# The residual kept by token: 512 moving weight columns per product, and seams pipelined by halves of the tokens

## The chip, the cores and the metric

The kernel runs on one core of a Trainium2 chip. The metric is the time of one execution on the device, in microseconds; several runs are taken and the median counts. A profiled execution gives the trace: TensorE (PE, with its weight loads as PEld), VectorE (DVE), ScalarE (ACT), GpSimd (POOL), and the queues of the DMA engines, most of whose transfers SyncE (SP) issues.

## What is computed

256 tokens of 1024 features go through two blocks, in float32. Cut to what matters:

```python
# block 1
h = swiglu(rms_norm(x, g1), w_in, w_out)            # 1024 -> 2 x 2816 -> 1024, silu(gate) * up
x = x + 0.5 * rms_norm(h, g2)
m = token_mixing(rms_norm(x, g3), ...)              # 4-head retention, 8-head neighbourhood attention, gates, projection
x = x + rms_norm(m, g4)
x = x + 0.5 * rms_norm(swiglu(rms_norm(x, g5), ...), g6)
# block 2, layers i = 0, 1 (0: causal attention of 16 heads; 1: differential attention of 8)
shift1, scale1, gate1, shift2, scale2, gate2 = split(silu(c) @ ada_w[i] + ada_b[i], 6)
y = attention(x * (1 + scale1) + shift1)
x = layer_norm(sqrt(2) * x + (1 + gate1) * y, ln_g[i, 0], ln_b[i, 0])
y = square(relu((x * (1 + scale2) + shift2) @ w_up[i])) @ w_down[i]      # 1024 -> 4096 -> 1024
x = layer_norm(sqrt(2) * x + (1 + gate2) * y, ln_g[i, 1], ln_b[i, 1])
```

The seven parts are FFN1, mixing, FFN2, attention 0, MLP 0, attention 1, MLP 1. What lies between two of them is called a seam here: a norm over the features of what the part gave, the new residual, and the input of the next part.

## The kernel before

**Products.** A float32 value is split into two float32r parts, high and low, and a product of two float32 matrices is three products of parts: high·high, low·high, high·low. All weights are streamed once: 198 slots of 1 MB, each in two halves. `Stream` loads a slot into `raw` (4 buffers, SP's queue), ACT copies a half into `wh` (line 109), DVE subtracts to get `wl` (line 90), and 7 halves of each can be in stock (RING). After each half slot that TensorE uses up, `tick()` emits the split of the next halves and advances the generators (`gens`) that hold the attention's and the sums' work, so that the order on every engine is that in which the program writes its instructions; nothing reorders them later. Instructions of an engine run in that order, and a waiting one holds up those behind it.

**Layout.** The residual X lies by features: [128 features, 8 chunks, 256 tokens], and nearly all products (`mmB`) hold a 128x128 block of weights stationary and move the 256 tokens (`g`, `u`, `q`, `k`, `acc` and so on: 48 products a slot). The values of attentions and mixing (`projA`) hold 128 tokens stationary and move 256 weight columns. In MLP up, after an attention, 258 columns are moved: two more columns carry what the norm's mean and shift add (`Ahead`).

**Seams.** Sums over the features run across partitions, so they are made with products against ones (`Stat.mms`, banks `pst`), after POOL or DVE have added six chunks; the factor 1/deviation (POOL's pow) is spread over partitions by two more products (`bcast`, banks `MU` and `R`); XH and XL, the parts of the next input, follow by chunks. Into these gaps the program puts one-column products of adaptive sums (`ada_mm`) and products that nobody reads (`warm`), both through `gap`. From an attention to its MLP the first products run before the statistics are known, on the unnormalized v.

**Adaptive sums.** silu(c) @ ada_w: 12 vectors of 1024, whose weights come as 48 more slots between the others. DVE adds up raw times a scalar (`adacc`, lines 317 and 320), then ACT and POOL make three bfloat16 parts (lines 331 to 337), and 24 one-column products (bank `adp`) add up the partitions. 9 of the 12 (HELD) have them in seams.

Of the kernel before, what the change touches and what calls it, by code (L numbers as in the profile page):

```python
# [16 lines left out]
D = 1024  # L17
S = 256
# [15 lines left out]
# the order of the parts of an attention (1 for queries and keys, 0 for values; of which heads), after how  # L34
# many steps of the stream a pair of heads starts, and from which pair on two of its steps are one
QKV = (((1, 0), (0, 0), (0, 1), (1, 1), (1, 2), (1, 3), (0, 2), (0, 3)),
       ((1, 0), (0, 0), (1, 1), (1, 2), (0, 1), (1, 3), (0, 2), (0, 3)))
WAITS = ((4, 5, 4, 3, 0, 5, 2, 1), (6, 5, 2, 4, 4, 4, 0, 2))
ONE = ((7, 8), (8, 6))
RET_WAITS = (1, 3, 4, 9)  # L40
NA_WAITS = (3, 2, 5, 4)

# the sums whose last products wait for the gap between two parts
HELD = (0, 1, 2, 4, 5, 6, 7, 9, 10)
# [5 lines left out]
class Stream:  # L50
    """Weights in the order of their use: loaded ahead, split into two float32r parts ahead."""
# [19 lines left out]
    def load(self, i, q=None):  # L71
# [3 lines left out]
        t = self.raw[i].rearrange("p (a b) -> p a b", b=s[2])  # L75
        if q is None:
            self.nc.sync.dma_start(t, s[1])
        else:
            n = t.shape[1] // 4
            self.nc.sync.dma_start(t[:, q * n:(q + 1) * n], s[1][:, q * n:(q + 1) * n])  # L80
# [41 lines left out]
    def quarter(self, n, q):  # L122
        """A quarter of slot n, the first of which come before any others."""
        h, c = q // 2, slice(q % 2 * 512, q % 2 * 512 + 512)
        if q % 2 == 0:
            self.parts[n, h] = tuple(self.pool.tile([128, 1024], F32R, name=i, bufs=RING) for i in ("wh", "wl"))
        wh, wl = self.parts[n, h]
        raw = self.raw[n][:, q * 512:(q + 1) * 512]
# [12 lines left out]
    def ahead(self):  # L141
        """The next half of a slot, when it is a weight's."""
# [3 lines left out]
    def use(self, n, b):  # L146
        """Slot n in two halves of its rows; each as its two parts, b columns wide."""
# [14 lines left out]
def block_kernel(ctx, tc, A, out):  # L162
# [22 lines left out]
    def rev(t):  # L185
        """[128, 2, 256] of a tile, every 64 of a row backwards."""
# [6 lines left out]
    # ---- small tensors  # L193
    xn = big.tile([128, 2, D], F32, name="xn", tag="P1")
# [5 lines left out]
    def first_loads(st):  # L200
        sy = nc.sync
        sy.dma_start(cst[:, 0:256], A["head"])
        for q in range(4):
            sy.dma_start(xn[:, :, q * 256:(q + 1) * 256], xv[:, :, q * 256:(q + 1) * 256])
            for i in range(2):
                st.load(i, q)
# [34 lines left out]
    def ffn_slots(w_in, w_out):  # L241
        def up(j):
            ws.append(cols(w_in, 256 * j))
            ws.append(cols(w_in, DFF + 256 * j))
        order(DFF // 256, up, lambda j: ws.append(rws(w_out, 256 * j)))

    def mlp_slots(w_up, w_dn):
        n = DFF2 // 256
        for j in range(n + 3):
# [7 lines left out]
    for i in range(2):  # L257
        ws.append(cols(wm, 256 * i))
        ws.append(cols(wm, 512 + 256 * i))
        for j in (2 * i, 2 * i + 1):  # L260
            ws.append(cols(wm, 1024 + 256 * j))
        for j in (2 * i, 2 * i + 1):
            ws.append(cols(wm, 2048 + 256 * j))
    for i in range(2):
        for b in (3072, 3584, 4096):
            ws.append(cols(wm, b + 256 * i))
    for i in range(4):
        ws.append(cols(wm, 4608 + 256 * i))
        ws.append(cols(A["w_ret_out"], 256 * i))
    for i in range(2):  # L270
        ws.append(cols(wm, 5632 + 512 * i))
        ws.append(cols(wm, 5632 + 512 * i + 256))
        ws.append(cols(A["w_na_out"], 512 * i, n=512))
# [3 lines left out]
    for l, (wi, wo) in enumerate((("moba_w_in", "moba_w_out"), ("diff_w_in", "diff_w_out"))):  # L277
        for f, i in QKV[l]:
            for b in ((0, D) if f else (2 * D,)):
# [1460 lines left out]
```

## Time and profile before

| | |
|---|---|
| median of 3 runs | 1287.63 us (1287.5 to 1288.11) |
| span of the profiled execution | 1287.8 us |
| TensorE busy | 1262.7 us, 98% |
| VectorE busy | 1046.8 us, 81% |
| ScalarE busy | 672.0 us, 52% |
| GpSimd busy | 280.5 us, 22% |
| read from memory | 262.56 MB, 205 GB/s over the span |

The profiled execution's span is all that is recorded of its time; it is the time that sums are made against. Busy shares are means over parts with different limits, so what a change is worth is read from the stretch in which it stands.

### The profile page before, as it was taken

Reading aid. Unit: us, or ns where it says so; the run is one execution under the profiler, and the core shown is the slowest. Engines: PE = TensorE matmul, PEld = TensorE weight load, DVE = VectorE, ACT = ScalarE, POOL = GpSimd, SP = SyncE. Lnnn points to the kernel's source line nnn. Section 1 sums busy time; section 2 is a strip of 40 time slices with the busy share of each in tenths; the row PEclk is TensorE's granted clock in tenths of the full one; section 3 lists DMA queues with packets and bytes.
Section 4 is the critical chain, followed back from the end, with each engine's and each line's share of the span. In section 5 each row is a group of like instructions: output and inputs, shape, how many; then the busy total and the mean of one; then the engine's idle time right before and its main releaser. Section 6 shows DMA issues by size and latency. Waiting matters only on the chain.

```text
span 1287.8 us, 25632 instructions
## 1 busy us (share of the span) xinstructions
PE 1262.7 (98%) x10768; PEld 1244.6 (97%) x10768; DVE 1046.8 (81%) x1437; ACT 672.0 (52%) x1070; POOL 280.5 (22%) x204
## 2 busy tenths in 40 slices
PE   9999999999999999999999999979999999999998
PEld 9999999999999999999999999979999999999997
DVE  5999867887776589887588759999969987998864
ACT  5454445656544365354465546545536565565542
POOL 1011104221000130011110017423322003832311
PEclk9999999999999999999999999989999999999999
DMA  8787974874566348877535335878753543677630
GB/s 300 264 309 256 317 244 90 268 240 149 200 226 212 116 164 301 303 279 262 164 111 186 131 99 188 270 271 281 260 171 113 183 132 103 225 250 234 202 134 33
DMA packets 176659, 265.25 MB, mean 206 GB/s; under 512 B 10432, under 2 KB 145952, under 8 KB 176544
## 3 DMA queue, kind: packets, MB, share of 16 engines
q1 hardware_dynamic: 169824, 261.53, 60.1%
q10 hardware_dynamic: 6720, 2.10, 0.9%
q8 instruction: 84, 1.38, 0.4%
q14 instruction: 31, 0.25, 0.1%
HBM read 262.56 MB, written 1.05 MB: 205 GB/s over the span
## 4 chain that ended last, share of the span: by engine, by line
PE 86%; DVE 8%; POOL 2%; issue 1%; ACT 1%; DMA 0%; DVEq 0%; SPq 0%; POOLq 0%; ACTq 0%
PE acc L191 24%; PE u L191 20%; PE g L191 12%; PE v L191 3%; PE q L191 3%; PE k L191 3%; PE oacc L191 2%; DVE wl L90 2%; PE yr L191 2%; PE rg L191 2%; PE rv L191 2%; PE as L191 1%; PE ao L191 1%; PE pst L191 1%; PE nk L191 1%
## 5 line engine op out<-in xcount | busy, mean ns | idle before, releaser
L90 DVE TENSOR_TENSOR wl<-raw,wh 128x1024 fp32r<-128x1024 f32 x392 | 515.2, 1334 | 24.3 <-ACT wh L109 23.9
L109 ACT ACTIVATE wh<-raw 128x1024 fp32r<-128x1024 f32 x392 | 403.6, 1052 | 130.3 <-PE u L191 32.2
L191 PE MATMUL acc<-HL,wh 128*128 128x256 f32 x864 | 243.9, 282 | 0.0
L191 PE MATMUL acc<-HH,wl 128*128 128x256 f32 x864 | 243.7, 282 | 0.0
L191 PE MATMUL acc<-HH,wh 128*128 128x256 f32 x864 | 242.8, 281 | 0.0
L191 PE MATMUL u<-XH,wh 128*128 128x258 f32 (+1 forms) x864 | 201.6, 285 | 0.4 <-ACT wh L129 0.4
L191 PE MATMUL u<-XL,wh 128*128 128x258 f32 (+1 forms) x864 | 200.7, 284 | 0.0
L191 PE MATMUL u<-XH,wl 128*128 128x258 f32 (+1 forms) x864 | 200.2, 283 | 0.0
L191 PEld LDWEIGHTS acc<-HH,wh 128*128 128x128 f32 x864 | 163.9, 190 | 0.0
L191 PEld LDWEIGHTS acc<-HH,wl 128*128 128x128 f32 x864 | 162.4, 188 | 0.0
L191 PEld LDWEIGHTS acc<-HL,wh 128*128 128x128 f32 x864 | 161.9, 187 | 0.0
L191 PEld LDWEIGHTS u<-XH,wh 128*128 128x128 f32 x864 | 145.7, 191 | 0.7 <-ACT wh L129 0.6
L191 PEld LDWEIGHTS u<-XH,wl 128*128 128x128 f32 x864 | 146.0, 191 | 0.1
L191 PEld LDWEIGHTS u<-XL,wh 128*128 128x128 f32 x864 | 145.1, 190 | 0.0
L191 PE MATMUL g<-XH,wh 128*128 128x256 f32 x480 | 133.5, 284 | 1.6 <-ACT XH L942 1.3
L191 PE MATMUL g<-XL,wh 128*128 128x256 f32 x480 | 133.2, 283 | 1.0 <-DVE XL L618 0.9
L191 PE MATMUL g<-XH,wl 128*128 128x256 f32 x480 | 132.7, 282 | 0.0
L320 DVE SCALAR_TENSOR_TENSOR adacc<-raw,csil,adacc 128x1024 f32<-128x1024 f32 x84 | 118.2, 1408 | 1.7
L834 POOL TENSOR_TENSOR a<-a,RB 128x512 f32<-128x512 f32 x32 | 68.0, 2125 | 170.7 <-DVE a L833 169.9
L333 POOL TENSOR_TENSOR adacc<-adacc,ada 128x1024 f32<-128x1024 f32 x12 | 27.7, 2311 | 329.3 <-ACT ada L331 254.3
L191 PEld LDWEIGHTS g<-XH,wh 128*128 128x128 f32 x480 | 89.5, 189 | 2.7 <-ACT XH L942 2.0
L191 PEld LDWEIGHTS g<-XL,wh 128*128 128x128 f32 x480 | 89.5, 189 | 1.6 <-DVE XL L618 1.1
(368 smaller groups left out, 2643.0 us busy)
## 6 DMA issues: line engine op xcount, KB each, us to landing
raw<-in_ada_w_dram SPq DMA_DIRECT2D x48, 1024.0 KB, 5.7
raw<-in_ffn_w_in_dram SPq DMA_DIRECT2D x42, 1024.0 KB, 6.8
raw<-in_mlp_w_up_dram SPq DMA_DIRECT2D x32, 1024.0 KB, 5.4
raw<-in_mlp_w_down_dram SPq DMA_DIRECT2D x32, 1024.0 KB, 5.0
raw<-in_w_mix_in_dram SPq DMA_DIRECT2D x26, 1024.0 KB, 5.6
raw<-in_ffn_w_out_dram SPq DMA_DIRECT2D x22, 1024.0 KB, 5.8
raw<-in_moba_w_in_dram SPq DMA_DIRECT2D x12, 1024.0 KB, 5.2
raw<-in_diff_w_in_dram SPq DMA_DIRECT2D x12, 1024.0 KB, 5.1
```

The costliest lines, as they stand in the source:

```text
L90: self.nc.vector.tensor_tensor(wl, raw, wh.bitcast(F32), OP.subtract)
L109: nc.scalar.activation(wh, self.raw[i][:, sl], AF.Copy)
L191: PE.matmul(o, l, r, start=start, stop=stop, skip_group_check=True)
L320: V.scalar_tensor_tensor(t, w, csil[:, kb:kb + 1], t, op0=OP.mult, op1=OP.add)
L333: GP.tensor_tensor(t, t, parts[0], OP.subtract)
L834: GP.tensor_tensor(two(t), two(t), bc2(self.R), OP.mult)
```

## The change

The residual now lies by token: X is [128 tokens, 2, 1024], and XX = [128 features, 8, 2 (high, low), 256] is the part's input, turned. Most products are now of one form, `mmA`: 128 tokens of an input stationary, 512 weight columns moving, 24 products a slot; slots are loaded as 512 columns of four chunks (`wide`), or 256 gate and 256 up columns (`both`). Queries, keys, the mixing's rq, rk, nq, nk, MLP up from block 2 on, and the late values of the attentions keep 256 columns. Sums over the features are now along a row: ACT's squares with a running sum (RMS), or DVE's `bn_stats` (layer norm). Gains, biases and gates that vary along a row come as rows broadcast by DMA (15 of 0.5 MB). Since hidden values are made by token, they are turned with TensorE transposes: 4 for a block of an FFN, 16 in an MLP, 16 in the mixing.

In a seam `down_tail` finishes token half 0 (accumulators (0, 0), (0, 1)), then half 1; `bank(t, f)` normalizes; `mid()` puts the transposes of half 0 (`turn(0)`, 8) where 6 products of half 1 are left; `projT` then does the next part's first 24 products for half 0, `turn(1)`, and 24 for half 1. `gap`, `warm` in seams, the statistics' products and `Ahead` are gone. Adaptive sums are emptied by `spare` within the parts: 8 of 12 as 24 one-column products, the 4 gates (s of 2 and 5) as 6 products of 512 columns that spread the sum over partitions. Their order among the weights, and the order and waits of the attentions' parts (QKV, WAITS, RET_WAITS), change too.

The core of the diff (of the new functions what is spoken of; what was removed is in the kernel above):

```diff
+QKV = (((2, 0), (1, 0), (1, 1), (1, 2), (1, 3), (0, 2), (0, 3)),
+       ((2, 0), (1, 0), (1, 1), (1, 2), (1, 3), (0, 2), (0, 3)))
+WAITS = ((0, 1, 0, 1, 0, 1, 0, 1), (0, 1, 0, 1, 0, 1, 0, 1))
 ONE = ((7, 8), (8, 6))
...
+    def wide(w, c0, k=KB):
+        return [("w", w[r:r + 512, c0:c0 + 512].rearrange("(k p) f -> p k f", p=128), 512) for r in range(0, 128 * k, 512)]
+    def both(w, c0):
+        v = w.rearrange("(k p) (g f) -> p k g f", p=128, g=2)
+        return [("w", v[:, k:k + 4, :, c0:c0 + 256], 512) for k in (0, 4)]
...
+    adas = [(l, s, i) for l, s in ((0, 0), (0, 1), (0, 3), (0, 4), (1, 0), (0, 2), (0, 5), (1, 1), (1, 3), (1, 4), (1, 2),
+                                   (1, 5)) for i in range(4)]
...
+    def spare(p):
+        if not ada_out:
+            return
+        l, s, parts, h = ada_out[0]
+        if s in (2, 5):
+            if h is None:
+                h = 0
+                g = grows[l, s] = late.tile([128, D], F32, name="grow", bufs=2)
+                src = A["ada_b"]
+                nc.sync.dma_start(g, bass.AP(tensor=src.tensor, offset=src.offset + (6 * l + s) * D, ap=[[0, 128], [1, D]]))
+            ada_out[0] = (l, s, parts, h + 1)
+            if h == 1:
+                ada_out.pop(0)
+            c = slice(512 * h, 512 * h + 512)
+            for i in range(3):
+                mm(p, onesb.to_broadcast([128, 128]), parts[i][:, c], i == 0, i == 2)
+            yield 1
+            g = grows[l, s][:, c]
...
+    def mmA(o, wh, wl, x, s, e):
+        mm(o, x[:, 0], wh, s, False)
+        mm(o, x[:, 0], wl, False, False)
+        mm(o, x[:, 1], wh, False, e)
+    TS = (slice(0, 128), slice(128, 256))
...
+    def projA(banks, X, nk=KB):
+        for i in range(nk // 4):
+            n = nxt()
+            for h, (wh, wl) in enumerate(st.use(n, 512)):
+                for t in range(2):
+                    for k in range(2):
+                        kk = 4 * i + 2 * h + k
+                        mmA(banks[t], wh[:, k], wl[:, k], X[:, kk, :, TS[t]], kk == 0, kk == nk - 1)
+                st.release(n, h)
+                tick()
+    def projT(banks, turn):
+        ns = [nxt(), nxt()]
+        w = []
+        for t in range(2):
+            turn(t)
+            for i in range(2):
+                if t == 0:
+                    w.append(st.use(ns[i], 512))
+                for h, (wh, wl) in enumerate(w[i]):
+                    for k in range(2):
+                        kk = 4 * i + 2 * h + k
+                        mmA(banks[t], wh[:, k], wl[:, k], XX[:, kk, :, TS[t]], kk == 0, kk == 7)
+                    if t:
+                        st.release(ns[i], h)
+                    if t or h:
+                        tick()
+    def down(accs, H, first):
         n = nxt()
         for kk, (wh, wl) in enumerate(st.use(n, D)):
+            for t in range(2):
+                for f in range(2):
+                    fs = slice(512 * f, 512 * f + 512)
+                    mmA(accs[t][f], wh[:, 0, fs], wl[:, 0, fs], H[:, kk, :, TS[t]], first and kk == 0, False)
             st.release(n, kk)
             tick()
+    def down_tail(accs, hs, post, mid):
         ns = [nxt(), nxt()]
         w = [st.use(n, D) for n in ns]
+        for t in range(2):
+            for f in range(2):
+                fs = slice(512 * f, 512 * f + 512)
+                for i in range(2):
+                    for kk in range(2):
+                        wh, wl = w[i][kk]
+                        mmA(accs[t][f], wh[:, 0, fs], wl[:, 0, fs], hs[i][:, kk, :, TS[t]], False, i == 1 and kk == 1)
+                    if t and f and i == 0:
+                        mid()
+                if t and f:
+                    for n in ns:
+                        for h in range(2):
+                            st.release(n, h)
+                post.bank(t, f)
+                if not (t and f):
+                    tick()
...
+    def turn_of(src, a, c, alloc=gu):
+        def turn(t):
+            for b in range(2):
+                p = alloc("xt")
+                for i in range(4):
+                    PE.transpose(p[:, i * 128:(i + 1) * 128], src[:, t, (4 * b + i) * 128:(4 * b + i + 1) * 128], ident)
+                f = None if c is None else w2("hf")
+                for i in range(4):
+                    k = 4 * b + i
+                    x, h, l = p[:, i * 128:(i + 1) * 128], XX[:, k, 0, TS[t]], XX[:, k, 1, TS[t]]
+                    if c is None:
+                        SC.activation(h, x, AF.Copy, scale=a[:, k:k + 1])
+                        V.scalar_tensor_tensor(l, x, a[:, k:k + 1], h.bitcast(F32), op0=OP.mult, op1=OP.subtract)
+                    else:
+                        ff = f[:, i * 128:(i + 1) * 128]
+                        SC.activation(h, x, AF.Identity, scale=a[:, k:k + 1], bias=c[:, k:k + 1])
+                        V.tensor_scalar(ff, x, a[:, k:k + 1], c[:, k:k + 1], op0=OP.mult, op1=OP.add)
+                        V.tensor_tensor(l, ff, h.bitcast(F32), OP.subtract)
...
     class PostRms:
+        def bank(self, t, f):
+            squares(self.s[:, t, f:f + 1], self.accs[t][f])
+            self.m[t, f] = w2("m")
+            V.tensor_tensor(self.m[t, f], self.accs[t][f], half(self.gain, f), OP.mult)
+            if f:
+                c = 1.0 / (self.coef * self.coef)
+                s = self.s[:, t, 0:1]
+                V.tensor_tensor(s, s, self.s[:, t, 1:2], OP.add)
+                r = rcol(s, c, D, self.eps)
+                for f in range(2):
+                    x = half(X[:, t], f)
+                    V.scalar_tensor_tensor(x, self.m.pop((t, f)), r, x, op0=OP.mult, op1=OP.add)
...
     class PostLn:
+        def bank(self, t, f):
+            v = half(self.v[:, t], f)
+            V.tensor_tensor(v, self.accs[t][f], half(self.gate, f), OP.mult)
+            V.scalar_tensor_tensor(v, half(X[:, t], f), ALPHA, v, op0=OP.mult, op1=OP.add)
+            V.bn_stats(self.s[:, t, f], v)
+            if f:
+                V.bn_aggr(self.mv[:, t], self.s[:, t].rearrange("p f s -> p (f s)"))
+                e = work.tile([128, 1], F32, name="ve", bufs=2)
+                V.tensor_scalar(e, self.mv[:, t, 1:2], 0.0, LN_EPS, op0=OP.max, op1=OP.add)
+                self.norm(t, self.mv[:, t, 0:1], rpow(e))
+        def norm(self, t, mu, r):
+            n = work.tile([128, 1], F32, name="nm", bufs=2)
+            V.scalar_tensor_tensor(n, mu, -1.0, r, op0=OP.mult, op1=OP.mult)
+            SC.activation(half(self.v[:, t], 0), half(self.v[:, t], 0), AF.Identity, scale=r, bias=n)
+            V.tensor_scalar(half(self.v[:, t], 1), half(self.v[:, t], 1), mu, r, op0=OP.subtract, op1=OP.mult)
...
+    def swiglu(cx, gain, first, post, mid):
...
+        def hidden(j, ps):
+            a, b = w2("a"), w2("b")
+            for t in range(2):
+                SC.activation(two(a)[:, t], ps[t][:, 0:256], AF.Silu, scale=r[0][:, t:t + 1])
+            for t in range(2):
+                V.scalar_tensor_tensor(two(b)[:, t], ps[t][:, 256:512], r[0][:, t:t + 1], two(a)[:, t],
+                                       op0=OP.mult, op1=OP.mult)
+            yield 1
+            p = ps[0]
+            for c in range(2):
+                for t in range(2):
+                    PE.transpose(two(p)[:, c, TS[t]], two(b)[:, t, c * 128:(c + 1) * 128], ident)
+            H = hp.tile([128, 2, 2, S], F32R, name="H", bufs=4)
+            split(H[:, :, 0], H[:, :, 1], two(p))
+            hid[j] = H
+            yield from spare(ps[1])
+            yield from spare(ps[0])
...
```

The first place is TensorE in FFN1, from the last product of block 2's projection into the first of its down product. Before (H is the hidden's two parts HH and HL, u the up projection):

```order
L191 MATMUL u<-XL,wh 128x256
L191 MATMUL u<-XH,wl 128x256
L191 MATMUL acc<-HH,wh 128x256
L191 MATMUL acc<-HL,wh 128x256
L191 MATMUL acc<-HH,wl 128x256
```

Of the change, at the same place (ps[0] and ps[1] are both named g; cst holds the identity):

```order
L197 MATMUL g<-wh,XX 128x512 x2
L197 MATMUL g<-wl,XX 128x512
L197 MATMUL g<-wh,XX 128x512
L197 MATMUL acc<-wh,H 128x512
...
L197 MATMUL acc<-wh,H 128x512
L695 MATMUL g<-cst,b 128x128 x4
L197 MATMUL acc<-wh,H 128x512
L197 MATMUL acc<-wl,H 128x512
```

Products have twice the columns, and four transposes of b stand in the middle of the down slot, 12 products behind the projection whose results they need.

The second place is VectorE in the seam from attention 0 to MLP 0 (oacc is the attention's output product, four banks; wl are low parts of the MLP's first weights). Before:

```order
L654 SCALAR_TENSOR_TENSOR v<-oacc,g_7816,X 128x256 x4
L761 SCALAR_TENSOR_TENSOR XL<-v,m00a,XH 128x256 x2
L777 TENSOR_TENSOR vs<-v 128x512
L90 TENSOR_TENSOR wl<-raw,wh 128x1024
L654 SCALAR_TENSOR_TENSOR v<-oacc,g_7816,X 128x256 x2
L761 SCALAR_TENSOR_TENSOR XL<-v,m00a,XH 128x256 x2
L779 TENSOR_TENSOR vs<-vs,v 128x512
...
L783 TENSOR_TENSOR ssum<-vs 128x256
L90 TENSOR_TENSOR wl<-raw,wh 128x1024 x3
```

Of the change, from the norm of half 0 on (hf and XX at lines 584 and 585 come 8 times each in turn):

```order
L631 SCALAR_TENSOR_TENSOR nm<-mv,r 128x1
L633 TENSOR_SCALAR v<-v,mv,r 128x512
L620 TENSOR_TENSOR v<-oacc,grow 128x512
L621 SCALAR_TENSOR_TENSOR v<-X,v 128x512
L622 BN_STATS bs<-v 128x6
...
L584 TENSOR_SCALAR hf<-xt,m00a,m00c 128x128
L585 TENSOR_TENSOR XX<-hf,XX 128x128
...
L620 TENSOR_TENSOR v<-oacc,grow 128x512
...
L633 TENSOR_SCALAR v<-v,mv,r 128x512
L96 TENSOR_TENSOR wl<-raw,wh 128x1024 x4
```

The second bank of half 1 now stands behind all of half 0's parts, and the next weights' low parts behind half 1's norm, which waits for POOL's pow; on ACT the order is the same (norm of half 1, then four copies `wh`).

## Rows read from the trace of the kernel before

**Rows 1.** The page: the span, each engine's busy time, the chain by engine.
```profile
span 1287.8 us, 25632 instructions
...
PE 1262.7 (98%) x10768; PEld 1244.6 (97%) x10768; DVE 1046.8 (81%) x1437; ACT 672.0 (52%) x1070; POOL 280.5 (22%) x204
...
PE 86%; DVE 8%; POOL 2%; issue 1%; ACT 1%; DMA 0%; DVEq 0%; SPq 0%; POOLq 0%; ACTq 0%
```

**Rows 2.** The chain in order of time, in FFN1: start, duration, engine, what.
```profile
46.20 5.68 PE acc L191 x48
51.88 5.70 PE g L191 x48
```

**Rows 3.** MLP 0's stall: TensorE's timeline, the chain, a window (columns as in rows 7).
```profile
845.46 0.74 PE L191 MATMUL adp<-small,ada 128*128 128x1 bf16 x22 [5.63 <-POOL ada L337]
...
846.20 5.14 PE u L191 x24
851.34 5.75 PE acc L191 x48
...
838.00:850.00 12.00, 5.42 (x48) 5.15 (x48) 11.89 (x13) 5.06 (x7) 5.24 (x2) 0.61 0.66 213
```

**Rows 4.** TensorE's timeline in mixing and its first seam; the tail's chain.
```profile
242.59 1.89 PE L191 MATMUL ry<-rv,dec 128*128 128x256 f32 x8
200.81 1.08 PE L191 MATMUL pst<-small,sq 128*128 128x64 f32 x8
...
1278.90 0.88 PE fo L863 x8
```

**Rows 5.** Seams: TensorE's timeline FFN1 to mixing, MLP 0 to attention 1; its waits.
```profile
199.71 0.66 PE L191 MATMUL pst<-small,ssum 128*128 128x64 f32 x4
204.91 0.47 PE L191 MATMUL rq<-XH,wh 128*128 128x256 f32 x2 [0.22 <-DVE XH L614]
207.03 0.51 PE L191 MATMUL rq<-XL,wh 128*128 128x256 f32 x2 [0.93 <-DVE XL L618]
...
966.33 1.24 PE L191 MATMUL pst<-small,ssum 128*128 128x64 f32 x8
972.42 0.50 PE L191 MATMUL q<-XH,wh 128*128 128x256 f32 x2
...
PE pst L191 <- DVE ssum L783: 1.9, 2, 1.0
```

**Rows 6.** Groups by line and form (busy, mean ns, idle before); two pieces of the chain.
```profile
L320 DVE SCALAR_TENSOR_TENSOR adacc<-raw,csil,adacc 128x1024 f32<-128x1024 f32 x84 | 118.2, 1408 | 1.7
L654 DVE SCALAR_TENSOR_TENSOR v<-oacc,g,X 128x256 f32<-128x256 f32 x16 | 7.0, 476 | 5.3 <-PE oacc L191 5.3
L1581 DVE TENSOR_SCALAR o<-ao,r 128x128 f32<-128x128 f32 x16 | 4.9, 347 | 0.3
...
L587 ACT ACTIVATE sq<-acc 128x512 f32<-128x512 f32 x9 | 5.4, 598 | 14.6 <-PE acc L191 14.6
L1276 ACT ACTIVATE ry<-ry,r 128x256 f32<-128x256 f32 x8 | 3.3, 464 | 1.8 <-POOL r L540 1.8
...
L337 POOL TENSOR_TENSOR ada<-adacc,ada 128x1024 bf16<-128x1024 f32 x12 | 33.1, 2756 | 30.1 <-ACT ada L335 30.1
L540 POOL TENSOR_TENSOR r<-s,small 128x2 f32<-128x2 f32 x18 | 18.0, 999 | 131.7 <-DVE s L545 121.4 <-DVE lr L1530 7.2 <-DVE r L1579 3.1
...
765.96 1.14 DVE wl L90
769.18 0.60 DVE vs L779
769.79 0.79 DVE v L654 x2
```

**Rows 7.** Window in FFN1: busy PE, PEld, DVE, ACT, POOL, clock, DMA share, GB/s.
```profile
60.00:90.00 30.00, 30.00 (x255) 30.00 (x254) 27.98 (x42) 17.18 (x21) 4.92 (x2) 1.00 0.90 317
```

**Rows 8.** The chain in order of time, at the program's end.
```profile
1276.27 2.62 PE pst L191 x24
```

More of the change, by code (lines that the diff above doesn't have):

```diff
@@ new lines, in block_kernel, with __init__, norm @@
+    class Last(PostLn):
+        def __init__(self, accs, gate, rows):
+            super().__init__(accs, gate)
+            self.rows = rows
+        def norm(self, t, mu, r):
+            g, b = self.rows
+            v = self.v[:, t]
+            for f in range(2):
+                V.scalar_tensor_tensor(half(v, f), half(v, f), mu, half(g, f), op0=OP.subtract, op1=OP.mult)
+            for f in range(2):
+                V.scalar_tensor_tensor(half(v, f), half(v, f), r, half(b, f), op0=OP.mult, op1=OP.add)
+                (SC if f else nc.sync).dma_start(out[t * 128:(t + 1) * 128, 512 * f:512 * f + 512], half(v, f))
@@ L1005, in swiglu, with __init__, token, close @@
+    class Rms:
+        def __init__(self):
+            self.s = work.tile([128, 2, 2], F32, name="s2", bufs=2)
+        def token(self, t):
+            for f in range(2):
+                squares(self.s[:, t, f:f + 1], half(X[:, t], f))
+        def close(self, c=1.0):
+            s = work.tile([128, 2], F32, name="s3", bufs=2)
+            V.tensor_tensor(s, self.s[:, :, 0], self.s[:, :, 1], OP.add)
+            self.r = rcol(s, c, D, RMS_EPS)
     @with_exitstack
-    def swiglu(cx, nx, gain, follow, pair=None):
+    def swiglu(cx, gain, first, post, mid):
@@ new lines, in swiglu @@
+        for j in range(n):
+            ps = [gu("g"), gu("g")]
+            if j == 0:
+                r[0] = first(ps)
+            else:
+                projA(ps, XX)
+            start_now(hidden(j, ps))
+            if j >= 2:
+                if accs is None:
+                    accs = [[acc("acc") for _ in range(2)] for _ in range(2)]
+                while j - 2 not in hid:
+                    tick()
+                down(accs, hid.pop(j - 2), j == 2)
+        while n - 1 not in hid:
+            bg()
@@ L1362, in mixing @@
[L1362 to L1378 removed]
+                    projA(bs, XX)
@@ new lines, in mixing @@
+            for i in range(2):
+                x = gates()
+                bs = [gu("yn"), gu("yn")]
+                projA(bs, N, 4)
+                for t in range(2):
+                    V.scalar_tensor_tensor(x[t], x[t], 1.0, bs[t], op0=OP.add, op1=OP.mult)
+                    V.tensor_tensor(half(T[:, t], i), half(T[:, t], i), x[t], OP.add)
+                start(turned(i), 1)
+            g = row(mp.tile([128, 3072], F32, name="grow", tag="bias")[:, 0:D], G_MPOST)
+            accs = [[acc("acc") for _ in range(2)] for _ in range(2)]
@@ L1622, in vv, with vw @@
                 vdone.add(i)
+            def vw(i):
+                bs = [gu("v"), gu("v")]
+                projT(bs, turn)
+                for t in range(2):
+                    SC.activation(half(vt[:, t], i), bs[t], AF.Copy)
+                vdone.update((2 * i, 2 * i + 1))
+                after()
             for f, i in QKV[l]:
```

1111 lines of the change are left out of this document (321 added, 790 removed).

## The prediction

> **What bounds the kernel now.** I read the page first: TensorE is busy for 1262.7 us of a span of 1287.8, and 86% of the chain that ended last is TensorE [rows 1]. The reader should see that nearly everything else is hidden under it, so a change counts by what it does to TensorE's own time and to its few waits. Then the chain in order of time, within a part: the slots follow one another without a gap, 48 products in 5.68 to 5.70 us, or 118.6 ns each, and about 5.75 in the second half of the program [rows 2, 3]. 198 such slots are 9504 products, about 1130 of the 1288 us. What is left lies in the seams between the parts (about 33 us, below), attention's small products, one stall [rows 3], the start, and a tail of 11.5 us from the end of the last weight product to the end of the span [rows 8]. The median of the runs shown is 1287.63, so the profiled time can stand for it.
>
> **Wide products.** In the changed kernel 142 of the 198 slots (all but MLP up from the third block on, attention's queries, keys and late values, and the mixing's rq, rk, nq, nk) are 24 products of 512 moving columns in place of 48 of 256: 3408 wide ones. No product of the trace has 512 columns in one pass. The nearest is the float32 product ry: it goes through in two passes over 256 columns, 512 column-steps; 8 take 1.89 us, and with 0.379 of it the latency of the last, 7 pitches are 216 ns [rows 4]. A second row bears on it: where the granted clock was down to 1.2 GHz (0.61 over the window with the wait), 24 products of 258 columns took 5.14 us, 214 ns each, which is 258 columns at 1.2 GHz and nothing on top [rows 3]. Against that, products of 64 columns have a pitch of 115 ns, and of 128 columns 110 [rows 4]: below some 110 ns a product gets no cheaper, however narrow. 256 columns at 2.4 GHz would stream in 107, so at 256 each product sits on this floor, at 118.6. I take 216 for 512. The lower bound is 213 (streaming alone). The upper is a fixed surplus per product, 118.6 − 107 = 12 on top of 213, so 225; or that nothing is gained, 235 to 237. At 216 each pair saves 237.2 − 216 = 21.2 ns: 3408 × 21.2 = **−72**. About 60 of the wide slots are those that now take 5.75, not 5.69 [rows 3]: **−3**.
>
> The Trainium skill ("TensorE: Matmul & The Clock Gate", section "Back-to-back issue gap") gives the isolated gap of a product as N/2.4 + 2.5 ns. That is 109.2 for 256 and 215.8 for 512: by it two narrow products cost hardly more than a wide one, and the change would gain 2.6 × 3408 = 9 us here, not 72. The trace disagrees at 256 (118.6) and agrees at 512 column-steps (216). The same section names 131 ns as sustained for 512; by that the change would save another 85 × 3408 = 290 us, and I give it no chance of its own beside the 216 of ry. By the isolated gap the time would be that of the width rival below, about 1319.
>
> **Turning.** Values are now made by token, so what the next product contracts over must be turned: 88 transposes in the two gated FFNs, 16 in the MLPs, 16 in the mixing, at 0.88 us for 8 [rows 4]: 120 × 0.109 = **+13**. Each set stands 12 products (2.6 us) behind the product that it waits for (order, below the diff); the work between is two ACT and two DVE instructions of 256 columns (0.46 and 0.48 from start to end [rows 6]), 1.6 to 2.5 us, hidden while DVE has no backlog.
>
> **Adaptive sums.** 12 sums of 24 one-column products are now done within the parts: 8 as before, and 4 as 6 products of 512 columns. 8 × 0.60 (22 of the 24 take 0.74 with the latency of the last [rows 3]) and 4 × 6 × 0.216 make 10.0 us; before, 9 of 12 sat in the seams, and the other three cost 1.8: **+8**. In exchange the stall goes: in MLP 0 TensorE waited 5.63 us for POOL's third part and about 1 ahead of it, then ran at 1.2 GHz, 24 products in 5.14 us where 24 × 0.119 = 2.85 is usual, 2.3 lost [rows 3]: **−9**.
>
> **Seams.** Before, a gated-FFN or mixing seam holds 5.2 us (the others 4.8 and 5.1) of statistics, sums and filling products between the last acc product and the first of the next part, then pauses [rows 5], 7 to 8 us in all; MLP to attention has 6.1; attention to MLP, which starts its products ahead of the statistics, only 16 of these products and a wait of 1, 2.9 twice. Sum: 33.
> After, each seam holds 16 transposes (1.75), 10.5 in all, and what the two token halves fail to hide. I walked each chain in the changed order from the moment T at which TensorE ends token half 0, with 24 products of half 1 (5.2 us) behind it.
> *RMS seams (3).* Half 0's X is ready at T + 3.8 (square 0.6 [rows 6] with the reading of its sum 0.8, add and scale 0.4, pow 1.0 [rows 6], two updates of 512 columns 1.3, small gaps), and its transposes, six products from the end of half 1, don't wait. But half 1's chain stands on DVE ahead of the fourth prepared half-slot's subtraction (1.14 [rows 6]). ACT makes 8 high parts of half 0 to T + 6.7, two squares of X to 7.9, then half 1's square to 8.6; DVE adds and scales to 9.0, pow to 10, X to 11.3, low parts of the weights to 12.5 and 13.6. The first 12 to 18 products of the new part end at T + 9; then TensorE waits to 12.5, does what is left and the transposes to 15.8, and starts half 1 at T + 16.0, where 24 + 24 products without a wait would start it at 10.4: 5.6 lost here, 5.2 and 6.5 in the two others, 17.3.
> *LayerNorm seams (3).* Here DVE does three instructions of 512 per bank (0.6 each [rows 6]), and all of half 0's parts stand before the second bank of half 1 (order, below the diff). Half 0: bank to T + 2.2, pow to 3.5, norm to 4.3. DVE goes on with bank (1, 0) to 6.1, four small ones to 6.8, 16 of 128 columns to 10.8 (0.35 from start to end; instructions of 256 columns take 0.48 and follow at 0.40 [rows 6], so about 0.25 apart), bank (1, 1) to 12.6, pow to 14.0. ACT's norm, which waits for this pow, ends at 14.7, its copy of the fourth half-slot at 15.7, DVE's subtraction at 16.9. TensorE has 18 products of the new part to T + 11.1; the last 6 wait to 15.7 and 16.9, so it stands for some 4.5 us. They end at 18.0, the transposes at 18.9, and DVE, with three more subtractions ahead, lets half 1 start at T + 20.4: 10.0 lost, 30.0 for three.
> After: 47.3; difference **+14**. In the stretch of rows 3 the granted clock fell after a wait of 5.6 us and stayed down for 24 products at a cost of 2.3. TensorE stands nearly as long in the LayerNorm seams, and its filling products are gone: 3 × 2.3 = **+7**.
>
> **Start and tail.** The start loses about 3 (the first gated result waits for its statistics); at the end the statistics products (2.62) go, and half 0's result leaves early: **0**.
> **Steady waits.** What I can't sum: DVE is busy for 28 of 30 us in the FFN's stretches with adaptive weights [rows 7], attention's rope (2.4 to 2.8 us) is just covered by 24 products, and spare sums wait for POOL's parts (2.8 for the third [rows 6]). Between 0 and 55 (below); I take 10, nearer to the low end since the subtractions on DVE are as many as before: **+10**.
> Sum: −72 − 3 + 13 + 8 − 9 + 14 + 7 + 10 = −32; 1287.8 − 32 = **1256**. For this case alone (steady waits 0 to 25, falls of the clock 0 to 12, P 213 to 219): 1238 to 1278. A measurement of this kernel can tell some 0.2%, or 2.6 us, from no change.
>
> **Rivals.**
> *The seams are hidden as meant* (0.17). For it: half 0's chain in the RMS seams does fit. Against it: the fourth half-slot's place in DVE's and ACT's order. Losses of some 4 us instead of 36.8, and no fall: 1256 − 33 − 7 = 1216.
> *Width gains nothing or little* (0.08). The surplus of 12 ns comes with the columns, not from a floor: at 225 the saving falls by 31 to 1287, at 235 by 63 to 1319. For it: 258 columns at 2.4 GHz cost 119 to 120, a little more than 256; against it ry's 216.
> *Other side: the gated blocks wait at their own transposes* (0.09). The place: DVE's two b instructions stand behind two adaptive sums (1.3 to 1.4 each [rows 6]) and pending subtractions in half of the blocks. If that backlog is the rule, each of 22 blocks waits 2.5 to 3.2 us, 55 to 70: about 1256 − 5 + 63 = 1314. It decides from 32/22 = 1.4 us per block.
> *The FFN's loads become the bound* (0.06). In the densest stretch the queues are busy for 0.90 at 317 GB/s [rows 7]. A block of three slots takes 17.07 us now and about 16.0 after, with transposes, so 338 GB/s, 0.96. If that isn't reached, some 16 us of the FFNs' gain is lost: about 1272.
> The main case has 0.60. Width's upper half and the blocks' waits are what lies above the range, and together with a little below the hidden seams they make 2 in 10: **1213 to 1284**. Faster by over 0.2%: 0.58 + 0.17 + 0.06 = 0.81; within it 0.04; slower 0.15.
>
> **What would show it.** Width: slots of 24 products at 5.2 us in the chain; 5.4 or 5.7 would refute the 216. Turning: transposes of g with no idle time before them; idle behind DVE's b is the other-side rival. Seams: in the LayerNorm ones TensorE idle for 4 to 5 us with the releaser wl or wh, then a granted clock below 1 in the windows; in the RMS ones 3 to 4 us behind wl. If the first u products behind a LayerNorm seam start their half 1 within 12 us of T, my order of waits is wrong. The stall of rows 3 should be absent. The prediction is wrong as a whole if the steady waits, which I chose and did not work out, exceed 25.

## The result

The changed kernel is slower: 1374.64 us (median of 4 runs, 1373.3 to 1379.57) beside 1287.87 (1287.5 to 1288.24), ratio 1.068 [1.066, 1.070]. The forecast was 1256, with a range of 1213 to 1284. The profiled execution has a span of 1377.8 us, 90.0 above that of before.

From its page, the span and the busy times:

```profile
span 1377.8 us, 18356 instructions
...
PE 1276.3 (93%) x7218; PEld 1081.7 (79%) x7222; DVE 968.7 (70%) x1348; ACT 655.3 (48%) x1032; POOL 134.2 (10%) x93
```

A third of TensorE's instructions is gone, and it is busy for longer than before; and it stands idle for 101 us, before for 25 [rows 1]. Both need an explanation: the first is mainly the price of a wide product, the second the waits.

Where the time went by part, in windows of the changed kernel that end with a part's last product (columns as in rows 7; FFN1, mixing, FFN2, attention 0, MLP 0, attention 1, MLP 1, tail):

```profile
0.00:203.90 203.90, 198.13 (x967) 162.36 (x968) 145.34 (x195) 105.26 (x143) 16.78 (x12) 0.99 0.80 270
203.90:448.60 244.70, 237.79 (x1342) 203.19 (x1341) 175.72 (x228) 128.34 (x209) 30.14 (x23) 0.98 0.62 198
448.60:661.70 213.10, 199.44 (x887) 159.69 (x889) 142.26 (x160) 100.76 (x138) 14.79 (x9) 0.97 0.68 230
661.70:792.50 130.80, 124.90 (x897) 110.93 (x895) 94.52 (x180) 65.58 (x145) 1.10 (x2) 0.97 0.42 137
792.50:1014.90 222.40, 200.02 (x1181) 172.97 (x1182) 157.59 (x180) 97.32 (x121) 28.14 (x16) 0.94 0.63 215
1014.90:1155.00 140.10, 121.49 (x825) 104.05 (x824) 114.29 (x240) 68.63 (x169) 22.41 (x18) 0.95 0.39 128
1155.00:1367.30 212.30, 194.57 (x1126) 168.48 (x1126) 132.40 (x155) 89.41 (x112) 19.89 (x12) 0.95 0.48 162
1367.30:1377.80 10.50, 0.00 (x0) 0.00 (x0) 6.58 (x12) 0.00 (x0) 0.99 (x1) 0.63 0.25 95
```

The same windows of before are 199.8, 245.0, 198.6, 126.0, 197.1, 120.1, 189.7 and 11.5 us long. So the parts changed by +4.1, −0.3, +14.5, +4.8, +25.3, +20.0, +22.6 and −1.0: 68 of the 90 us lie in the three parts that begin with a LayerNorm seam, and nearly nothing was gained where no long wait stands.

What TensorE waits for most (total, times, longest):

```profile
PE u L197 <- ACT wh L115: 15.1, 2, 7.5
PE u L197 <- DVE q L747: 13.8, 6, 2.4
PE g L695 <- DVE b L689: 10.7, 5, 3.7
PE v L197 <- ACT wh L115: 9.7, 2, 7.5
PE rv L197 <- DVE wl L96: 6.9, 1, 6.9
```

The timeline of the changed kernel: two rows of TensorE in FFN1, 39 products apart; then the seam from attention 0 to MLP 0, where token half 0 ends at 785.5 (TensorE; VectorE, with one row of the first RMS seam ahead; ScalarE; GpSimd); then one adaptive sum in MLP 0.

```profile
72.75 0.62 PE L197 MATMUL g<-wh,XX 128*128 128x512 f32 x2
81.59 0.40 PE L197 MATMUL g<-wh,XX 128*128 128x512 f32 x1
...
805.94 0.79 PE L197 MATMUL u<-wh,XX 128*128 128x512 f32 x1 [7.52 <-ACT wh L115]
815.96 0.73 PE L197 MATMUL u<-wh,XX 128*128 128x512 f32 x2 [2.79 <-DVE XX L585]
818.34 0.63 PE L197 MATMUL u<-wl,XX 128*128 128x512 f32 x1
819.62 0.63 PE L197 MATMUL u<-wl,XX 128*128 128x512 f32 x1
823.25 0.40 PE L197 MATMUL u<-XX,wh 128*128 128x256 f32 x2
...
204.15 0.35 DVE L580 SCALAR_TENSOR_TENSOR XX<-xt,sm,XX 128x128 fp32r<-128x128 f32 x1 [0.43 <-ACT XX L579]
797.13 0.41 DVE L584 TENSOR_SCALAR hf<-xt,m00a,m00c 128x128 f32<-128x128 f32 x1 [0.20 <-ACT XX L583]
798.07 0.41 DVE L584 TENSOR_SCALAR hf<-xt,m00a,m00c 128x128 f32<-128x128 f32 x1 [0.20 <-ACT XX L583]
805.92 8.72 DVE L96 TENSOR_TENSOR wl<-raw,wh 128x1024 fp32r<-128x1024 f32 x4 [1.37 <-ACT wh L115]
...
797.57 0.46 ACT L583 ACTIVATE XX<-xt,m00c,m00a 128x128 fp32r<-128x128 f32 x1 [0.48 <-DVE hf L584]
804.85 3.88 ACT L115 ACTIVATE wh<-raw 128x1024 fp32r<-128x1024 f32 x4
...
806.99 2.14 POOL L641 TENSOR_TENSOR X<-X,lnb 128x512 f32<-128x512 f32 x1
...
873.19 0.74 PE L197 MATMUL u<-small,ada 128*128 128x1 bf16 x24 [2.29 <-DVE q L747]
```

The reader is to see: a wide product costs (81.59 − 72.75)/39 = 227 ns, not 216. In the seam, from 785.5 to 823.25 are 37.8 us for 72 wide products and 16 transposes, which need 72 × 0.2305 + 1.74 = 18.3 (0.2305 is the middle between 227 in the projections and 231 to 237 in down products): 19.5 are lost. VectorE's hf and ScalarE's XX, which read the same bank and don't need each other's result, wait for each other (0.93 to 0.94 us a chunk), and four wl take 2.18 each while GpSimd works on the residual. In the RMS seams the two engines alternate as well, 0.79 a chunk, but there VectorE does need ScalarE's high part.

### The profile page after: what moved, and what is told of

Same layout as the page of the kernel before. It is cut to its first block, busy times and chain, and to the rows that moved or that the text cites. A ratio compares the mean times of both kernels' runs of the same rounds, so it can differ in the third digit from the quotient of the medians.

```text
span 1377.8 us, 18356 instructions
## 1 busy us (share of the span) xinstructions
PE 1276.3 (93%) x7218; PEld 1081.7 (79%) x7222; DVE 968.7 (70%) x1348; ACT 655.3 (48%) x1032; POOL 134.2 (10%) x93
## 5 line engine op out<-in xcount | busy, mean ns | idle before, releaser
L197 PE MATMUL acc<-wh,H 128*128 128x512 f32 x864 | 291.1, 406 | 0.0
L197 PE MATMUL g<-wh,XX 128*128 128x512 f32 x832 | 267.4, 396 | 2.5 <-ACT wh L115 2.5
L197 PEld LDWEIGHTS acc<-wh,H 128*128 128x128 f32 x864 | 167.3, 194 | 40.5 <-issue 0.3
L197 PEld LDWEIGHTS g<-wh,XX 128*128 128x128 f32 x832 | 158.3, 190 | 37.3 <-ACT wh L115 2.9
L197 PE MATMUL acc<-wl,H 128*128 128x512 f32 x432 | 176.0, 407 | 0.0
L197 PE MATMUL g<-wl,XX 128*128 128x512 f32 x416 | 164.4, 395 | 2.5 <-DVE wl L96 2.5
L197 PE MATMUL u<-XX,wh 128*128 128x256 f32 x896 | 162.3, 283 | 0.0
L197 PEld LDWEIGHTS u<-XX,wh 128*128 128x128 f32 x896 | 141.1, 191 | 2.3
L197 PE MATMUL u<-XX,wl 128*128 128x256 f32 x448 | 126.6, 283 | 0.0
L197 PEld LDWEIGHTS u<-XX,wl 128*128 128x128 f32 x448 | 85.7, 191 | 0.0
L345 POOL TENSOR_TENSOR adacc<-adacc,ada 128x1024 f32<-128x1024 f32 x12 | 26.5, 2212 | 522.6 <-ACT ada L343 522.6
L534 POOL TENSOR_TENSOR r<-s,small 128x2 f32<-128x2 f32 (+1 forms) x21 | 18.3, 871 | 340.8 <-DVE s L539 340.8
L197 PE MATMUL u<-wh,XX 128*128 128x512 f32 x64 | 27.8, 504 | 21.7 <-ACT wh L115 15.1
```

What stands on the lines that cost most here:

```text
L197: PE.matmul(o, l, r, start=start, stop=stop, skip_group_check=True)
L345: GP.tensor_tensor(t, t, parts[0], OP.subtract)
L534: GP.tensor_tensor(r, s, mhalf[:, 0:s.shape[1]], OP.pow)
```

## The experiments

All change the changed kernel ("the seam" below is that from attention 0 to MLP 0). The kernel before took 1287.9 us beside the changed kernel and 1288.2 to 1289.7 beside the runs below, and the runs of one version lie up to 8.5 us apart, so a difference of 2 us between two medians decides nothing.

**The fourth half-slot earlier.**

```diff
                     if t and f and i == 0:
                         mid()
+                        for h in range(2):
+                            st.release(ns[0], h)
+                        st.ahead()
+                        st.flush()
```

> Edit: in each seam the next part's fourth half-slot is split ahead of half 1's second bank (its ring place is released as soon as its last reader has run), so it no longer stands behind half 1's norm on ACT and DVE. Place theory (the prediction's): the waits for wh and wl in the seams (3 x 8.8, 6.9, 5.0, 4.9 us, 43 in all) and most of the half-clock stretches behind them go, 40 us or more, 1335 or below. Chain theory: in a LayerNorm seam VectorE's own chain from the end of token half 0 to the last low part of half 1 takes 37 us (eight chunks at 0.93 us, low parts of weights at 2.2 us), and the wait only moves from wh to XX: 3 us a LayerNorm seam, 3 to 5 an RMS seam, 1350 to 1362.

Measured: 1379.7 (1374.55 to 1382.68), no gain. TensorE's timeline in the seam:

```profile
800.99 0.51 PE L197 MATMUL u<-wh,XX 128*128 128x512 f32 x1 [1.54 <-ACT wh L115]
807.46 1.97 PE L576 MATMUL xt<-cst,v 128*128 128x128 f32 x8 [3.77 <-ACT v L635]
816.20 1.22 PE L197 MATMUL u<-wh,XX 128*128 128x512 f32 x2 [4.33 <-DVE XX L588]
```

The wait of 7.5 us is cut up and stands again at the transposes and low parts; from the end of half 0 the seam takes 37.1 us in place of 37.8. My place theory falls. Of the chain theory it holds that the wait moves to XX; its gain does not come.

**Adaptive sums later in an MLP block.**

```diff
             V.tensor_tensor(q, q, p, OP.mult)
-            yield from spare(p)
             yield 1
             split(*tile_of(j), two(q))
+            yield from spare(p)
```

> Edit: in an MLP block the adaptive sum's products come after the split of the hidden values, one half-slot later, and go to the same bank. Bank theory: the six waits of 2.3 us (13.8) are for VectorE's reading of the product that has just ended in that bank; they go, and with them the half-clock stretches behind five of them (20 us at half speed, some 8 lost): about 1352. POOL theory (the prediction's: sums wait for their third part): the waits stay, no change within 3 us, 1372 to 1378.

Measured: 1356.52 (1355.02 to 1357.76), 18 us faster, and the six waits are gone. The sum's bank is the one whose product had just ended, so its 24 products waited for ScalarE's and VectorE's reading of it. The later place would hide a wait for GpSimd's third part too, so the edit alone does not separate the two theories; the trace of the changed kernel does. At three of the six sums that part had ended 6.6 to 16.9 us earlier (at the others 0.9), and TensorE waited 2.3 us at all six: the bank theory holds.

**The width undone.**

```diff
-        mm(o, x[:, 0], wh, s, False)
-        mm(o, x[:, 0], wl, False, False)
-        mm(o, x[:, 1], wh, False, e)
+        for xx, w, ss, ee in ((x[:, 0], wh, s, False), (x[:, 0], wl, False, False), (x[:, 1], wh, False, e)):
...
+            mm(o[:, 0:n], xx, w[:, 0:n], ss, ee)
+            mm(o[:, n:2 * n], xx, w[:, n:2 * n], False, ee)
```

> Edit: every product of 512 columns is issued as two of 256, all else as in the changed kernel. By the trace (227 to 237 ns for 512, 118 to 120 for 256) the width saves 2 x 119 - 230.5 = 8 ns on 3408 products, 27 us; undone where TensorE doesn't wait anyway, +20 to +27: 1395 to 1402. By the prediction's 216 it would be +72, 1447. If the width itself were what makes the change slower, the time would fall below 1370.

Measured: 1394.32 (1390.66 to 1397.64), +20 against 1374.6. The width gains, but 20 us and not 72.

**Products by themselves.** A kernel of its own: `for i in range(n): PE.matmul(o[:, 0:cols], s, m, ...)` for eight forms.

> Only products, on parts of x, in a row, 96 to 144 of a form, twice over (VectorE copies beside the first forms); the output is x and nothing of the reference is computed. Forms: 128, 256, 384 and 512 moving columns in float32r; 256 and 512 with 64 rows; 512 with one stationary block for all; 512 in bfloat16. Fixed-surplus theory: a float32r product costs its columns at 2.4 GHz plus 12 to 14 ns whatever the width: 119, 173, 227. Floor theory (the prediction's): 512 costs 214 to 216 and only 256 and below sit above their streaming time. Placement theory: 227 here and 231 to 237 in the down products come from where operands lie, so all rows here agree with 227. If the surplus belongs to the change of the stationary block, one block for all gives 214; if to its rows, 64 rows give 214 to 216.

Measured, by line and form (c: 128 rows; r: 64 rows; s: one stationary block; b: bfloat16); each group is two runs of its form, and two ends of 0.16 us are to be taken off:

```profile
L196 PE MATMUL c<-wr,xs 128*128 128x512 f32 x192 | 44.3, 391 | 0.0
L196 PE MATMUL s<-wr,xs 128*128 128x512 f32 x192 | 44.2, 391 | 0.0
L196 PE MATMUL r<-wr,xs 64*128 64x512 f32 x192 | 44.1, 387 | 0.0
L196 PE MATMUL b<-wb,xb 128*128 128x512 bf16 x192 | 41.8, 379 | 0.0
L196 PE MATMUL c<-wr,xs 128*128 128x256 f32 x288 | 34.9, 283 | 0.0
L196 PE MATMUL c<-wr,xs 128*128 128x384 f32 x192 | 33.6, 334 | 0.0
L196 PE MATMUL c<-wr,xs 128*128 128x128 f32 x288 | 32.4, 275 | 0.0
```

(44.3 − 0.33)/192 = 229 ns for 512 columns, 173 for 384, 120 for 256, 111 for 128; 228 with one block or 64 rows; 216 in bfloat16. So at the full clock a float32r product costs its columns at 2.4 GHz and 13 to 16 ns on top, whatever the width from 256 on; neither a new stationary block nor its number of rows makes it. The block was loaded ahead of every product in each form, also where it stayed the same, so what the load itself costs is not shown. The fixed-surplus theory holds, but for the full clock only: in the seam above, three wide products at 1.2 GHz take 1.28 us (818.34 to 819.62), 427 ns each, and 512 columns at 1.2 GHz are 427, with nothing on top. What makes the surplus stays open, and so do the 231 to 237 of the down products, which it does not explain. The Trainium skill ("TensorE: Matmul & The Clock Gate", "Back-to-back issue gap") gives N/2.4 + 2.5, 215.8 for 512: the bfloat16 form agrees (216), the float32r forms do not (229), and there the measurement decides.

**The turn without alternation.**

```diff
+                if c is not None:
+                    for i in range(4):
+                        k = 4 * b + i
+                        V.tensor_scalar(f[:, i * 128:(i + 1) * 128], p[:, i * 128:(i + 1) * 128], a[:, k:k + 1],
+                                        c[:, k:k + 1], op0=OP.mult, op1=OP.add)
...
-                        SC.activation(h, x, AF.Identity, scale=a[:, k:k + 1], bias=c[:, k:k + 1])
-                        V.tensor_scalar(ff, x, a[:, k:k + 1], c[:, k:k + 1], op0=OP.mult, op1=OP.add)
+                        SC.activation(h, ff, AF.Copy)
                         V.tensor_tensor(l, ff, h.bitcast(F32), OP.subtract)
```

> Edit: in a turn with scale and shift VectorE first makes the four chunks of a bank, and ScalarE makes the high parts from VectorE's result, not from the bank; the same number of instructions. In the changed kernel ScalarE and VectorE read the four chunks of one PSUM bank strictly in turn (each waits for the other, 0.93 us a chunk), though neither needs the other's result for it. Alternation theory: a chunk comes down to 0.5 to 0.7 us, both halves' chains get 2 to 3 us shorter, 3 to 5 us a LayerNorm seam: 1358 to 1366. If the 0.93 is the instructions' own time: no change within 4 us.

Measured: 1358.19 (1354.83 to 1363.29), 16 us faster. VectorE's timeline in the seam:

```profile
789.13 1.37 DVE L578 TENSOR_SCALAR hf<-xt,m00a,m00c 128x128 f32<-128x128 f32 x4
790.42 0.89 DVE L589 TENSOR_TENSOR XX<-hf,XX 128x128 fp32r<-128x128 f32 x4
791.22 1.36 DVE L578 TENSOR_SCALAR hf<-xt,m00a,m00c 128x128 f32<-128x128 f32 x4
```

Four chunks in 2.1 us, 0.52 a chunk, with the same number of instructions: the alternation theory holds. The edit takes ScalarE off the bank and also lets VectorE go four chunks ahead; which of the two ended the waiting, this run does not separate.

**The residual held back.**

```diff
+            last = XX[:, 7, 1, S - 1:S].bitcast(F32)
+            GP.tensor_tensor(hold, last, last, OP.add)
```

> Edit: a one-column instruction ahead of the residual's eight on GpSimd reads the last low part of half 1, so that the residual is computed after the seam and not in it. Port theory: the four subtractions wl of a LayerNorm seam took 2.2 us each while GpSimd computed on 512 columns, and 1.15 alone; without it half 1's low parts come 4 us earlier in each of three seams: 1360 to 1364. If the 2.2 us have another cause (loads, ScalarE): no change, 1370 to 1378.

Measured: 1369.8 (1366.85 to 1372.8), 5 us below the changed kernel, less than expected. VectorE in the seam, and GpSimd behind it:

```profile
800.71 4.63 DVE L96 TENSOR_TENSOR wl<-raw,wh 128x1024 fp32r<-128x1024 f32 x4 [1.37 <-ACT wh L115]
813.10 5.67 DVE L96 TENSOR_TENSOR wl<-raw,wh 128x1024 fp32r<-128x1024 f32 x3 [0.21 <-ACT wh L115]
...
813.12 2.35 POOL L642 TENSOR_TENSOR X<-v,lng 128x512 f32<-128x512 f32 x1
```

The four subtractions come down from 8.72 to 4.63 us, so GpSimd was their cause; but the next three now take 5.67 beside it. From the attention's last product to the MLP's first down product are 44.2 us, before the edit 44.6: the collision moved. The two profiled executions lie 6.8 us apart; 3.6 of it is in FFN2, which the edit does not touch, and the three parts behind a LayerNorm seam change by −1.6, +2.2 and −3.1. So by itself the edit shows what slows the subtractions, and hardly a gain in time. The Trainium skill ("SBUF — State Buffer", "SBUF: two separate sides") says that VectorE and GpSimd share a pair of ports, which one of them holds for a whole instruction; the rows agree (2.18 us for a subtraction beside GpSimd's work, 1.16 without).

**Filling products in the seams.** `warm(banks[1], 130)` ahead of the last 6 products of half 0, and 45 behind the second transposes (LayerNorm seams; 85 or 120 in RMS seams).

> Edit: in front of the waiting products of each seam 85 to 130 bfloat16 products that nobody reads, and 45 behind the second transposes of the LayerNorm seams; the waits stay as long as they were. Clock theory: the half-clock stretches behind the seams' waits (65 us in all at 1.2 GHz, of which some 20 are lost) go, the others (MLP sums, FFN blocks) stay: 1350 to 1358. If the clock falls for another reason than TensorE standing: same stretches, same time or longer.

Measured: 1372.45 (1369.23 to 1374.17), 2 us less, which the spread of the runs covers. The mean granted clock rose:

```profile
core 0: 1369.0 us, clock 0.987
```

from 0.963; so (0.037 − 0.013) × 2 × 1370, some 66 us, are no longer at 1.2 GHz. TensorE's timeline in the seam:

```profile
791.69 7.43 PE L197 MATMUL u<-identb 128*128 128x128 bf16 x130
809.42 0.73 PE L197 MATMUL u<-wh,XX 128*128 128x512 f32 x2 [2.60 <-DVE XX L589]
816.84 0.40 PE L197 MATMUL u<-XX,wh 128*128 128x256 f32 x2
```

The seam's first product stands at 786.2 here, so it is 30.6 us to 816.84; in the changed kernel 792.74 to 823.25, 30.5. At full speed half 1's products would have waited for VectorE: a chunk's low part comes every 0.93 us, and the three products that need it take 0.68. So the clock does fall behind these waits, and it costs next to nothing there. My price for it was wrong.

**Three of them together** (sums, turn, residual).

> The later sums of the second run, the turn without alternation and the held residual together, without filling products. If they are separate causes their gains add up: 18 + 14 + 12 below the changed kernel, 1328 to 1334; more if waits get short enough for the clock to stay up; less if they shorten the same chain only up to the next wait (ScalarE's copy behind the norm): 1340 or above.

Measured: 1332.24 (1329.24 to 1333.93); 18 + 16 + 5 = 39 expected from the single runs, 42 found: they add up within the spread.

**Three half-slots behind the turn.** On top of the combined version, `if t or h: tick()` in projT becomes `if t: tick()`.

> The combined version (later sums, turn without alternation, held residual; 1332 us) with one more edit: the splitting of three further half-slots, which stood between half 1's norm and half 1's turn on ScalarE and VectorE, comes behind that turn. Chain theory: VectorE's chain from the end of half 0 to half 1's last low part gets shorter by two subtractions of 1.15 us, and TensorE's end of the seam follows one to one in the three LayerNorm seams, less in the RMS seams: 7 to 10 us, 1322 to 1326. If something else set the seam's end (TensorE's clock, the weights' low parts): no change, or longer by the subtractions that now come later.

Measured: 1347.1 (1346.17 to 1349.76), 15 slower; the chain theory, as I put it, falls. TensorE's timeline:

```profile
797.72 0.65 PE L197 MATMUL u<-wl,XX 128*128 128x512 f32 x1 [4.80 <-DVE wl L96]
...
818.97 2.35 PE L747 MATMUL u<-cst,q 128*128 128x128 f32 x8 [6.57 <-DVE q L742]
```

The second transposes stand behind half 0's products, and 11 of these wait 4.8 us for a low part of the third half-slot, which is still made behind half 1's norm; half 1 starts 21.6 us after the end of half 0, as in the combined version. And the deferred subtractions then stand ahead of q, the MLP's first hidden values: the waits for q come to 13.1 us, in the combined version to 4.5.

**The fourth half-slot earlier on top of it**, and one ScalarE and one VectorE instruction for four chunks' parts (`split(ys[:, :, 0], ys[:, :, 1], ...)`).

> The version before it, with the fourth half-slot split ahead of half 1's bank (the edit of the first run, which gave nothing by itself) and the high and low parts of four chunks made by one instruction each. Chain theory: no subtraction of weights is left between half 1's norm and its turn, and eight small instructions are four fewer a half: another 2 to 3 us a LayerNorm seam and 3 to 5 us in the RMS seams, 1308 to 1318. If the place of the fourth half-slot doesn't matter (as in the first run): only the grouping shows, 1318 to 1324.

Measured: 1338.58 (1334.99 to 1340.1), 8.5 below the last and above the combined version; neither theory gave this. The waits for q come to 8.8 us in place of 13.1, but from the end of half 0 the three LayerNorm seams take 1 to 2 us longer than in the last version (28.6 to 29.9 us, against 27.4 to 28.2).

**Hidden values turned one half-slot later**, on top of it: in the gated block `yield 1` ahead of the transposes becomes `yield 2`.

> The version before it, with the transposes of a gated block's hidden values one half-slot later (24 products behind the projection, not 12). Backlog theory (the prediction's rival in small): TensorE's waits for VectorE's b in FFN1 and FFN2 (7 to 10 us in 5 places) go, with two half-clock stretches: 8 to 11 us. If the b instructions are late for a whole slot: the same waits elsewhere, no change.

Measured: 1327.78 (1326.12 to 1328.49), 11 faster, with no wait for b left in the list: the backlog theory holds. This is the fastest version, 3.0% [2.9, 3.2] above the kernel before.

**All edits, with the three half-slots at their first place.**

> All edits that helped, with the three half-slots split where the changed kernel has them: later sums, turn without alternation and with grouped parts, held residual, fourth half-slot ahead of half 1's bank, transposes of hidden values one half-slot later. Work theory: a seam's length is the amount of VectorE's work between the end of half 0 and the first results of the next part, and deferring subtractions only moves the wait behind them; so against the last run the time falls again by what deferring cost (about 10), to 1314 to 1320. Place theory (each subtraction counts where it stands ahead of half 1's turn): 1328 to 1336, no better than the last run. Either way the kernel before, at 1288, isn't reached: half the gain of the width is missing and the LayerNorm seams still cost 8 to 12 us more each.

Measured: 1332.11 (1331.97 to 1333.04), which is what the place theory gave. But two edits pull against each other here: the grouped parts make VectorE wait 0.69 us for ScalarE's copy twice a half, so that half 1's last low part follows half 0's by 15.5 us, against 14.0 in the combined version without grouping; and the longest wait for q is 1.1 us, against 4.2 in the run before. What the place of the three subtractions is worth by itself is not settled by these runs.

## Why the prediction was wrong

**Wide products: the step "I take 216 for 512".** The nearest row was that of ry [rows 4], a plain float32 product; the weights' products are float32r, and these carry 13 to 16 ns each that ry does not have. The right reading lay in rows 2: 118.6 − 107 = 12 at 256 columns as a fixed surplus, which I put down as the upper bound (225); the measured 227 to 237 lies above even that. The floor at 110 ns is there for float32r at 128 columns (111) and had no part in the 118.6; nor does it hold "however narrow", since the one-column bfloat16 products of rows 3 follow one another at some 28 ns ((0.74 − 0.16)/21). The term of −75 is −20 by the run with the width undone (−27 by the pitches alone): 55 us.

**LayerNorm seams: the step "about 0.25 apart".** The order of instructions showed which stand ahead of which, but I priced the sixteen small ones as a row of one engine's. They alternate with ScalarE over one bank, 0.93 a chunk where I had 0.50: the chain to half 1's bank is 3.4 us longer, and so is the chain to half 1's own low parts. Then GpSimd's residual, which I had not placed, stretched the subtractions ahead of half 1 from 4.6 to 8.7 us. Half 1 starts at T + 26.5 and goes on at T + 30.5 in place of T + 20.4. The 10.0 that I had as lost counts the transposes too; by that sum this seam loses 37.8 − 72 × 0.2305 = 21.2 us and the two others 20.9 each: 33 more than the 30.0 of the prediction. In the combined version, without the alternation and with the residual held back, the same three lose 11.4, 11.0 and 11.0, close to the forecast: these two make nearly all of the 33.

**RMS seams: the step "ACT makes 8 high parts of half 0 to T + 6.7".** I priced ScalarE's high parts as a row of its own here too. They alternate with VectorE's low parts, 0.79 a chunk, and end at T + 10.2; TensorE then stands for 6.9 us behind a low part of the third half-slot, and half 1 starts at T + 23.0 in place of T + 16.0. From the end of half 0 to the end of the 72 products the three seams take 28.9, 26.2 and 27.8 us (the first from 197.3 to 226.2), so they lose 12.3, 9.6 and 11.2 where I had 17.3 in all: 16 more. No run took this alternation away, so its share of the 16 is argued and not shown.

**Seam order.** That the fourth half-slot is late was right, and the wait of 7.5 us for it is in the trace; that it is the cause was wrong. Taken away by itself, it uncovers the chain behind it.

**Steady waits: the step "I take 10".** The sums in the MLP cost 18 us, not for GpSimd's parts, as I had it, but for their bank; the gated blocks cost 11. I named the second as a rival with a backlog in every block; it appears in 5 places, 10.7 us. Together they make 29, more than the 25 above which the prediction called itself wrong as a whole.

**Clock.** It fell as foreseen behind waits, more often than foreseen; in the seams that cost some 2 us at most, not 7, since TensorE was not what set their length.

**What held.** The old stall is gone; the tail is about as long as before (10.5 against 11.5); the width gains something; FFN1 and the mixing change little (+4.1, −0.3).

The pieces 55 + 33 + 16 + 18 + 11 make 133, and 17 of these were allowed for (waits and clock), which leaves 116; the miss is 119. They come from different runs and from one trace, so that they nearly meet is partly luck: the terms for the transposes and the adaptive sums were not measured by themselves, nor were attention 1's waits for rope and o (5 us of TensorE idle).

## What to carry to other kernels

Take the price of an instruction from a row of the same data type, even if its shape is farther off, and check it against the fixed surplus in the rows at hand. When two engines read one bank, price the chain as strictly alternating until a row shows otherwise, and ask of every product that is put into a bank who still reads it. A seam that was hidden by filler work and is now pipelined by halves has the other engines' whole work on its path: add up all that VectorE does from the first half's end to the next part's first result, with GpSimd's work beside it, before judging the order.

## What the runs showed of the hardware

A float32r product of 256 to 512 columns costs 13 to 16 ns above its columns at 2.4 GHz (229 ns for 512), with the same stationary block or a new one, loaded each time; a bfloat16 one of 512 columns costs 3 (216 ns). At 1.2 GHz the float32r surplus is gone: 427 ns for 512 columns, 214 for 258 [rows 3]. A VectorE subtraction of 1024 columns takes 1.16 us alone and 2.18 beside GpSimd's work on 512 columns. TensorE's granted clock was down to 1.2 GHz for some 100 us of the changed kernel (0.963 over the span), and taking two thirds of that away changed the time by 2 us, within the spread of the runs.
